# Copying the products of a seven-product matmul pair out with ScalarE and joining them as side work

## The chip, the core and the metric

The kernel runs on one core of one Trainium2 chip. A core has a matrix engine (PE, TensorE), two element-wise engines that matter here (DVE is VectorE, ACT is ScalarE), a third one (POOL, GpSimd) that does little here besides starting some transfers, and SP (SyncE), which only starts transfers between the chip's large memory and the on-chip memory SBUF. PE writes its results to PSUM, a small memory of eight banks; DVE and ACT read them from there. Each engine works through its own instructions strictly in order, and waits at an instruction until the semaphores that it needs have been raised.

The metric is the time of one execution in microseconds (us). Lower is better.

## The reference

Two layers of a hybrid decoder trunk on x of 512 positions by 2048 features, in fp32. Cut to what matters:

```python
for l in range(DEPTH):                                  # DEPTH = 2
    h = rms_norm(x, pre_norm_g[l])
    proj = jnp.einsum('bsd,de->bse', h, w_in[l])        # 2048 -> 6656
    (rq, rk, rv, rg, dq, dk, dv, dg, lx, lg) = jnp.split(proj, split_idx, axis=-1)
    ret_out  = rms_norm(retention(rq, rk, rv)) * silu(rg)               # 768 wide
    diff_out = rms_norm(diff_attention(dq, dk, dv), g) * c * silu(dg)   # 512 wide
    lru_out  = rg_lru(lx) * silu(lg)                                    # 768 wide
    mixed = jnp.concatenate([ret_out, diff_out, lru_out], axis=-1)
    y = jnp.einsum('bse,ed->bsd', mixed, w_out[l])      # 2048 -> 2048
    x = x + rms_norm(y, post_norm_g[l])
```

## The kernel before

**Products.** A matmul takes operands in a reduced fp32 format (fp32r), so every weight and activation is held as two parts, `hi` and `lo`, and one product is three matmuls: hi by hi, hi by lo, lo by hi. A weight chunk comes from memory as `raw` (128 partitions by 1024 values, 512 KB), ACT casts it to `whi` (line 190), and DVE subtracts that from `raw` to get `wlo` (line 191). `raw`, `whi` and `wlo` have three buffers each. So the buffer for the `raw` of a chunk is free only when the `wlo` of the third chunk before it has been made.

**Order of the work.** Each layer has 13 passes of the input projection, and then the output projection in four parts: pass 13 is the first 512 output columns (four PSUM banks), part 14 is the Pair (output columns 512 to 1535), and the two last passes are the last 512 columns, two banks each. `run_pass` and `run_pair` emit the matmuls (lines 296 and 370). Before each of them `ensure(i)` steps the weight chunks on: a chunk is a generator with a load, an addition (in the Pair only) and a split, and the additions run 2 chunks ahead of the splits, the loads 4. All else (norms, attention, the next layer's preparation) is side work: generators in a queue `side`, of which `pump()` runs one step between matmuls. SP's instructions run in the order in which the program wrote them; the other engines' are ordered by a scheduler by priority, and evacuations and chunk steps carry a raised priority (`HP`).

**The Pair.** The 1024 output columns are computed with seven products of half-size blocks in place of eight (the scheme of Strassen and Winograd). There are 28 units, numbered from 0: four of A11·B11, then, for four parts c, S1·T1 and S3·T3 by turns, then S2·T2 and S4·B22, then A12·B21 and A22·T4. One unit is 12 matmuls, and each product fills two PSUM banks (t = 0 and 1). The weight sides T1 to T4 are sums of weight blocks: DVE adds a `raw` to `wx` (line 230), and for S3·T3 POOL starts a transfer that adds to a `raw` in place (line 234). The activation sides S1 to S4 are made by `Sums` from `mf`, full-precision copies of the mixed activations (lines 396, 406, and 386/387 for their split). At the last part of each product `evac` takes the PSUM banks: three products are copied to SBUF by ACT (line 338), the four others are combined by DVE straight out of PSUM (lines 341, 345, 351 and 354, with 346 to 348 in SBUF). `o1`/`o2` are `out_y`: a sum of squares by ACT (line 990) and a product with the norm's weight by DVE (line 997).

**The end of a layer.** `finish` (line 1016, DVE) adds the residual `xr` to the scaled result. In the first layer it is followed by the preparation of the next layer's input: PE transposes (line 1024), ACT `hhi` (1031), DVE `hlo` (1032). The residual comes by 16 loads of 256 KB each, `load_x` (line 977), which are side work that is put in the queue at the unit (A12·B21, 0). Their tiles come from the pool `U` (77 tiles of 128 by 512).

**Turned tiles.** `diff_final` (from line 755) turns the attention's output by PE transposes into PSUM, ACT makes `mhi` from it (768), DVE `mlo` (769), and ACT makes `mf`, the same values again in plain fp32 (771).

Of the kernel before, what the change touches and what calls it, by code (L numbers as in the profile page):

```python
# [17 lines left out]
AF = mybir.ActivationFunctionType  # L18
ALU = mybir.AluOpType
# [19 lines left out]
ADD, LOAD = 2, 4  # L39
# [10 lines left out]
K_LRU, K_RET, K_DIFF = 0, 6, 12  # L50
# [63 lines left out]
A11_B11, A12_B21, S1_T1, S2_T2, S4_B22, S3_T3, A22_T4 = range(7)  # L114
# [6 lines left out]
def tile_hybrid_trunk(ctx, tc, x, xt, pos, ppar, lamqk, w_in, gw, w_out, postg, cp, cm, out):  # L121
    nc = tc.nc
# [18 lines left out]
    def U(s, dt=F32):  # L141
        return up.tile([P, S], dt, tag="u", name=nm(s))
# [70 lines left out]
    def load_unit(i):  # L213
        p, (s, c) = chunk_list[i]
        w1, w2 = p.w
        if s == A11_B11:
            src = p.x[c] = [U("wx"), U("wx")]
            for kk in range(2):
                nc.sync.dma_start(src[kk], w1[c][:, kk * S:(kk + 1) * S])
        elif s == S1_T1:  # L220
            p.kept[c] = load_raw(w2[c])
        elif s == S2_T2:
            p.kept[c] = load_raw(w2[c + 4])
        elif s == A12_B21:
            p.kept[c] = load_raw(w1[c + 4])
        yield
        if s in (S1_T1, S2_T2, A22_T4):
            src = p.x[c]
            for kk in range(2):
                V.tensor_tensor(src[kk], src[kk], p.kept[c][:, kk, :], op=ALU.add)  # L230
        elif s != A11_B11:
            src = p.kept[c]
        if s == S3_T3:
            nc.gpsimd.dma_start(src, w2[c + 4].rearrange("p (k c) -> p k c", k=2), accum_op=ALU.add)
        yield
        hi, lo = split_tiles()
        if isinstance(src, list):
            for kk in range(2):
                split(hi[:, kk, :], lo[:, kk, :], src[kk])
        else:  # L240
            split(hi, lo, src)
        chunk_tiles[i] = (hi, lo)
        yield


    def ensure(i):
        for step, more in enumerate((LOAD, ADD, 0)):
            while loaded[step] <= min(i + more, len(chunk_list) - 1):
                n = loaded[step]
                if n not in steps:  # L250
                    steps[n] = (load_unit if isinstance(chunk_list[n][0], Pair) else load_chunk)(n)
                with tc.high_priority(HP):
                    next(steps[n])
                loaded[step] += 1
# [63 lines left out]
        for c in range(nch):  # L318
            del chunk_tiles[base + c]

    def run_pair(p, begin):
        base = cbase[0]
        cbase[0] += len(UNITS)
        ps, p1, p5, p7 = {}, {}, {}, {}
        lo_, hi_ = slice(0, 256), slice(256, 512)

        def stationary(s, c, kk, part):
            if s in SUM_OF:
                return p.sums.parts[SUM_OF[s], c][part][:, kk * 256:(kk + 1) * 256]
            k = 2 * c + kk + (0 if s == A11_B11 else 8)  # L330
            return p.act[k][part][:, hi_ if s == A22_T4 else lo_]

        def evac(s, t, x):
            o1, o2 = p.out
            if s in (A11_B11, S1_T1, S3_T3):
                held = {A11_B11: p1, S1_T1: p5, S3_T3: p7}[s]
                held[t] = U("held")
                A.copy(held[t], x)
            elif s == A12_B21:
                e = U("e")  # L340
                V.tensor_tensor(e, x, p1[t], op=ALU.add)
                o1(t, e)
            elif s == S2_T2:
                w, e = U("w"), U("e")
                V.tensor_tensor(w, x, p1[t], op=ALU.subtract)
                V.tensor_tensor(p5[t], p5[t], w, op=ALU.add)
                V.tensor_tensor(e, p5[t], p7[t], op=ALU.subtract)
                V.tensor_tensor(p7[t], p7[t], w, op=ALU.subtract)
                o2(2 + t, e)
            elif s == S4_B22:  # L350
                V.tensor_tensor(p5[t], x, p5[t], op=ALU.add)
                o2(t, p5.pop(t))
            else:
                V.tensor_tensor(p7[t], x, p7[t], op=ALU.add)
                o1(2 + t, p7.pop(t))

        for n, (s, c) in enumerate(UNITS):
            if (s, c) in begin:
                side.append(begin[s, c]())
            if s in SUM_OF:  # L360
                until(lambda: (SUM_OF[s], c) in p.sums.parts)
            ensure(base + n + 2)
            hi, lo = chunk_tiles.pop(base + n)
            for t in range(2):
                if c == 0:
                    ps[s, t] = pb.tile([P, S], F32, tag="big", name=nm("big"))
                for kk in range(2):
                    ah, al = (stationary(s, c, kk, part)[:, t * P:(t + 1) * P] for part in range(2))
                    for m, (wt, at) in enumerate(((hi, ah), (hi, al), (lo, ah))):
                        T.matmul(ps[s, t], lhsT=at, rhs=wt[:, kk, :], start=(c == kk == m == 0),  # L370
                                 stop=(c == 3 and kk == 1 and m == 2))
                if c == 3:
                    with tc.high_priority(HP):
                        evac(s, t, ps.pop((s, t)))
            pump()


    class Sums:
# [10 lines left out]

        def make(self, c):  # L390
            f, plain = self.f, self.plain
            for k in (2 * c, 2 * c + 1):
                if k not in f:
                    f[k] = U("mf")
                    hi, lo = self.act[k]
                    V.tensor_tensor(f[k], hi.bitcast(F32), lo.bitcast(F32), op=ALU.add)
# [16 lines left out]
                del f[k]  # L413

        def all(self):
            for c in (0, 1, 3, 2):
                yield from self.make(c)
                yield
# [340 lines left out]
    def diff_final(l, st):  # L759
        for tb in range(NT):  # L760
            V.tensor_tensor(st["dod"][tb], st["dod"][tb], st["dg"][tb], op=ALU.mult)
        yield
        for h in range(DIFF_H):
            ps = SM("dT")
            for tb in range(NT):
                T.transpose(ps[:, tb * P:(tb + 1) * P], st["dod"][tb][:, h * P:(h + 1) * P], ident)
            hi, lo = U("mhi", F32R), U("mlo", F32R)
            A.activation(hi, ps, AF.Identity, scale=subg[:, l:l + 1])
            V.scalar_tensor_tensor(lo, ps, subg[:, l:l + 1], hi, op0=ALU.mult, op1=ALU.subtract)
            m = st["mf"][K_DIFF + h] = U("mf")  # L770
            A.activation(m, ps, AF.Identity, scale=subg[:, l:l + 1])
            st["mix"][K_DIFF + h] = (hi, lo)
            yield

# [381 lines left out]
    for l in range(DEPTH):  # L1156
# [5 lines left out]
        for i, (p, tasks) in enumerate(layer_passes[l]):  # L1162
# [4 lines left out]
                st["pg"][n] = U("pg")  # L1167
                nc.sync.dma_start(st["pg"][n], postg[l, n * S:(n + 1) * S].partition_broadcast(P))
            if isinstance(p, Pair):
                run_pair(p, {(S1_T1, 1): st["sums"].rest, (A12_B21, 0): lambda l=l, st=st: load_x(l, st)})  # L1170
            else:
                run_pass(p)
            for t in tasks:
# [98 lines left out]
```

## Time and profile before

| | us |
|---|---|
| Median of three runs (1648.52 to 1648.67) | 1648.53 |
| The profiled execution's own time | 1647.76 |
| Its span, first to last instruction | 1646.0 |
| PE busy | 1613.4 |
| DVE busy | 1048.5 |
| ACT busy | 710.4 |
| POOL busy | 66.2 |
| Mean granted clock of PE | 0.993 of full speed |
| Data moved | 181.70 MB, 110 GB/s on average |

The profile shows one execution. PE is busy in all but 32.6 us of the span, so what can be had at its present work is in these 32.6 us and in the stretches where its clock was granted at less than full speed. A row of the timeline gives the start, the duration, the engine, the line and the operation (out <- in), and in brackets how long the engine had been idle and what released it. A row of the windows gives a stretch, its length, and for each engine the busy time and the number of instructions, then the granted clock, the share of the transfer engines, and GB/s. "SPq" is SP's instruction queue.

### The profile page before, as it was taken

Reading aid. Unit: us, or ns where it says so; the run is one execution under the profiler, and the core shown is the slowest. Engines: PE = TensorE matmul, PEld = TensorE weight load, DVE = VectorE, ACT = ScalarE, POOL = GpSimd, SP = SyncE. Lnnn points to the kernel's source line nnn. Section 1 sums busy time; section 2 is a strip of 40 time slices with the busy share of each in tenths; the row PEclk is TensorE's granted clock in tenths of the full one; section 3 lists DMA queues with packets and bytes.
Section 4 is the critical chain, followed back from the end, with each engine's and each line's share of the span. In section 5 each row is a group of like instructions: output and inputs, shape, how many; then the busy total and the mean of one; then the engine's idle time right before and its main releaser. Section 6 shows DMA issues by size and latency. Waiting matters only on the chain.

```text
span 1646.0 us, 19583 instructions
## 1 busy us (share of the span) xinstructions
PE 1613.4 (98%) x7445; PEld 1326.6 (81%) x7445; DVE 1048.5 (64%) x1798; ACT 710.4 (43%) x1134; POOL 66.2 (4%) x92
## 2 busy tenths in 40 slices
PE   9999999999999999999799999999999999999997
PEld 7888888878888887877588888887888888878776
DVE  7747746557586456868662774655757744458686
ACT  7233333456732235444552343434673222435442
POOL 1010000000000000000120000000000000000001
PEclk9999999999999999999899999999999999999998
DMA  6333332223233222446543232222323322234466
GB/s 229 122 99 100 93 100 65 84 89 98 77 101 94 75 78 97 116 113 227 189 158 98 90 103 90 77 72 89 97 79 100 103 65 77 90 102 123 115 221 220
DMA packets 57053, 181.70 MB, mean 110 GB/s; under 512 B 6912, under 2 KB 7936, under 8 KB 56960
## 3 DMA queue, kind: packets, MB, share of 16 engines
q1 hardware_dynamic: 53744, 169.94, 32.3%
q0 software_dynamic: 3072, 10.49, 2.5%
q8 instruction: 58, 0.95, 0.2%
q14 instruction: 35, 0.29, 0.1%
q10 hardware_dynamic: 144, 0.04, 0.0%
HBM read 172.05 MB, written 8.39 MB: 110 GB/s over the span
## 4 chain that ended last, share of the span: by engine, by line
PE 87%; DVE 6%; issue 3%; DMA 2%; ACT 2%; POOL 0%; DVEq 0%; POOLq 0%; ACTq 0%
PE big L296 75%; PE big L370 4%; DMA raw<-in_w_out 2%; DVE wlo L191 2%; PE gate L815 1%; PE acc L706 1%; ACT whi L190 1%; PE ro L909 1%; PE rs L884 1%; PE sc L673 1%; PE sc L674 1%; PE wT L696 1%; PE ro L912 0%; PE kv L898 0%; DVE wx L230 0%
## 5 line engine op out<-in xcount | busy, mean ns | idle before, releaser
L191 DVE TENSOR_TENSOR wlo<-raw,whi 128x1024 fp32r<-128x1024 f32 (+1 forms) x281 | 340.6, 1218 | 320.1 <-ACT whi L190 315.5
L190 ACT CAST whi<-raw 128x1024 fp32r<-128x1024 f32 (+1 forms) x281 | 293.2, 1047 | 485.3 <-PE big L296 319.1
L296 PE MATMUL big<-hhi,whi 128*128 128x512 f32 x1024 | 401.8, 393 | 0.0
L296 PE MATMUL big<-hhi,wlo 128*128 128x512 f32 x1024 | 399.1, 390 | 0.0
L296 PE MATMUL big<-hlo,whi 128*128 128x512 f32 x1024 | 398.9, 390 | 0.0
L296 PE MATMUL big<-whi,hhi 128*128 128x512 f32 x640 | 253.3, 398 | 0.0
L296 PE MATMUL big<-whi,hlo 128*128 128x512 f32 x640 | 249.9, 390 | 0.0
L296 PE MATMUL big<-wlo,hhi 128*128 128x512 f32 x640 | 249.8, 391 | 0.0
L296 PEld LDWEIGHTS big<-hhi,wlo 128*128 128x128 f32 x1024 | 192.2, 188 | 40.5
L296 PEld LDWEIGHTS big<-hhi,whi 128*128 128x128 f32 x1024 | 192.5, 188 | 39.4
L296 PEld LDWEIGHTS big<-hlo,whi 128*128 128x128 f32 x1024 | 192.4, 188 | 38.8
L296 PEld LDWEIGHTS big<-wlo,hhi 128*128 128x128 f32 x640 | 120.2, 188 | 26.2 <-DVE wlo L191 0.5
L296 PEld LDWEIGHTS big<-whi,hhi 128*128 128x128 f32 x640 | 120.5, 188 | 24.1 <-ACT whi L190 1.0
L296 PEld LDWEIGHTS big<-whi,hlo 128*128 128x128 f32 x640 | 120.5, 188 | 23.8
L296 PE MATMUL big<-whi,mhi 128*128 128x512 f32 x256 | 102.4, 401 | 6.7 <-ACT whi L190 6.7
L296 PE MATMUL big<-wlo,mhi 128*128 128x512 f32 x256 | 100.6, 400 | 3.4 <-DVE wlo L191 3.2
L296 PE MATMUL big<-whi,mlo 128*128 128x512 f32 x256 | 101.2, 396 | 0.0
L682 ACT ACTIVATE pr<-sc,mx 128x128 f32<-128x128 f32 (+3 forms) x64 | 33.2, 523 | 86.6 <-DVE mx L679 86.6
L296 PEld LDWEIGHTS big<-whi,mhi 128*128 128x128 f32 x256 | 49.1, 192 | 18.1 <-ACT whi L190 8.5
L296 PEld LDWEIGHTS big<-wlo,mhi 128*128 128x128 f32 x256 | 49.3, 192 | 16.6 <-DVE wlo L191 6.3
L296 PEld LDWEIGHTS big<-whi,mlo 128*128 128x128 f32 x256 | 49.1, 192 | 9.9
L370 PE MATMUL big<-wlo,sh 128*128 128x512 f32 x128 | 50.5, 395 | 3.3 <-DVE wlo L191 3.3
(264 smaller groups left out, 1945.0 us busy)
## 6 DMA issues: line engine op xcount, KB each, us to landing
raw<-in_w_in SPq DMA_DIRECT2D x207, 512.0 KB, 3.6
raw<-in_w_out SPq DMA_DIRECT2D x72, 512.0 KB, 3.8
xT<-in_xt SPq DMA_DIRECT2D x16, 256.0 KB, 6.6
wx<-in_w_out SPq DMA_DIRECT2D x16, 256.0 KB, 4.3
raw<-in_w_out POOLq DMA_DIRECT2D x8, 512.0 KB, 6.1
xr<-in_x SPq DMA_DIRECT2D x16, 256.0 KB, 6.1
xr<-xs SPq DMA_DIRECT2D x16, 256.0 KB, 6.6
pg<-in_postg SPq DMA_DIRECT2D x8, 256.0 KB, 3.9
```

Source lines behind the costliest of these rows:

```text
L190: last_copy[0] = A.copy(hi, raw)
L191: V.tensor_tensor(lo, raw, hi, op=ALU.subtract)
L296: T.matmul(ps[b], lhsT=lhsT, rhs=rhs, start=(cnt[b] == 0), stop=(cnt[b] == total - 1))
L370: T.matmul(ps[s, t], lhsT=at, rhs=wt[:, kk, :], start=(c == kk == m == 0), stop=(c == 3 and kk == 1 and m == 2))
L673: T.matmul(ps[:, :n], lhsT=qs[:, blk], rhs=ks[:, :n], start=True, stop=False)
L674: T.matmul(ps[:, :n], lhsT=qs[:, blk], rhs=kl[:, :n], start=False, stop=True)
L682: A.activation(p[:, :n], sc[c][:, :n], AF.Exp, bias=mx[:, c:c + 1], scale=0.125, accum_out=sums[:, h:h + 1])
L696: T.transpose(ps[:, kb * P:(kb + 1) * P], w[:, kb * P:(kb + 1) * P], ident)
L706: T.matmul(accs[i][:, h * P:(h + 1) * P], lhsT=wt[:, kb * P:(kb + 1) * P], rhs=dv[kb][:, h * P:(h + 1) * P], start=(kb == 0), stop=(kb == i))
L815: T.matmul(ps[:BW, :], lhsT=wt[:BW, cols], rhs=at[:BW, :], start=(n == 0), stop=(n == 2))
L884: T.matmul(ps[:, n * P:(n + 1) * P], lhsT=k[:, n * P:(n + 1) * P], rhs=q[:, n * P:(n + 1) * P], start=True, stop=True)
L909: T.matmul(po[:, n * P:(n + 1) * P], lhsT=sT[:, n * P:(n + 1) * P], rhs=v[:, n * P:(n + 1) * P], start=True, stop=(n == 0))
```

## The change

Five things are changed, in both layers.

1. All seven products of the Pair are copied out of PSUM by ACT (`held`). They are joined by DVE from SBUF, in three generators that go to the side queue after the units number 11, 19 and 27.
2. The 16 residual loads are emitted one by one, one after each unit from number 12 on, and are no longer side work.
3. `ensure` emits the split of the chunk that is needed first, then the additions of later chunks, then the loads.
4. The transfer that adds in place is emitted at the addition step of S1·T1, not of S3·T3, on the same tile.
5. `diff_final` no longer makes `mf`; `Sums.make` makes it by a DVE addition of hi and lo. `Sums.all` begins with an empty step.

```diff
-        if s == S3_T3:
-            nc.gpsimd.dma_start(src, w2[c + 4].rearrange("p (k c) -> p k c", k=2), accum_op=ALU.add)
+        if s == S1_T1:
+            nc.gpsimd.dma_start(p.kept[c], w2[c + 4].rearrange("p (k c) -> p k c", k=2), accum_op=ALU.add)
...
-        for step, more in enumerate((LOAD, ADD, 0)):
+        for step, more in ((0, 0), (1, 0), (2, 0), (0, ADD), (1, ADD), (0, LOAD)):
...
-    def run_pair(p, begin):
+    def run_pair(p, begin, loads):
...
-        def evac(s, t, x):
-            o1, o2 = p.out
-            if s in (A11_B11, S1_T1, S3_T3):
-                held = {A11_B11: p1, S1_T1: p5, S3_T3: p7}[s]
-                held[t] = U("held")
-                A.copy(held[t], x)
-            elif s == A12_B21:
-                e = U("e")
-                V.tensor_tensor(e, x, p1[t], op=ALU.add)
-                o1(t, e)
-            elif s == S2_T2:
-                w, e = U("w"), U("e")
-                V.tensor_tensor(w, x, p1[t], op=ALU.subtract)
-                V.tensor_tensor(p5[t], p5[t], w, op=ALU.add)
-                V.tensor_tensor(e, p5[t], p7[t], op=ALU.subtract)
-                V.tensor_tensor(p7[t], p7[t], w, op=ALU.subtract)
-                o2(2 + t, e)
-            elif s == S4_B22:
-                V.tensor_tensor(p5[t], x, p5[t], op=ALU.add)
-                o2(t, p5.pop(t))
-            else:
-                V.tensor_tensor(p7[t], x, p7[t], op=ALU.add)
-                o1(2 + t, p7.pop(t))
+        held, left = {s: {} for s in range(7)}, {}
+        o1, o2 = p.out
+        def join_first():
+            p1, p5, p7 = held[A11_B11], held[S1_T1], held[S3_T3]
+            for t in range(2):
+                V.tensor_tensor(p5[t], p5[t], p1[t], op=ALU.subtract)
+                yield
+                left[t] = U("held")
+                V.tensor_tensor(left[t], p7[t], p1[t], op=ALU.add)
+                yield
+        def join_right():
+            p2, p3, p5, p7 = held[S2_T2], held[S4_B22], held[S1_T1], held[S3_T3]
+            for t in range(2):
+                V.tensor_tensor(p5[t], p5[t], p2[t], op=ALU.add)
+                V.tensor_tensor(p3[t], p3[t], p5[t], op=ALU.add)
+                yield
+                V.tensor_tensor(p5[t], p5[t], p7.pop(t), op=ALU.subtract)
+                V.tensor_tensor(left[t], left[t], p2.pop(t), op=ALU.subtract)
+                yield
+            for t in range(2):
+                o2(t, p3.pop(t))
+                yield
+                o2(2 + t, p5.pop(t))
+                yield
+        def join_left():
...
                 if c == 3:
+                    held[s][t] = U("held")
                     with tc.high_priority(HP):
-                        evac(s, t, ps.pop((s, t)))
+                        A.copy(held[s][t], ps.pop((s, t)))
+            if n in (11, 19, 27):
+                side.append({11: join_first, 19: join_right, 27: join_left}[n]())
+            if n > 11:
+                next(loads)
             pump()
...
-            for k in (2 * c, 2 * c + 1):
+            for k in (2 * c, 2 * c + 1, 2 * c + 8, 2 * c + 9):
...
         def all(self):
+            yield
...
-            m = st["mf"][K_DIFF + h] = U("mf")
-            A.activation(m, ps, AF.Identity, scale=subg[:, l:l + 1])
...
-                run_pair(p, {(S1_T1, 1): st["sums"].rest, (A12_B21, 0): lambda l=l, st=st: load_x(l, st)})
+                run_pair(p, {(S1_T1, 1): st["sums"].rest}, load_x(l, st))
```

How the instructions move, at three places. All names are the kernel's; the number behind a name counts tiles. After the change the lines have other numbers: 386 and 387 are 405 and 406, 396 is 415, 768 and 769 are 788 and 789, 977 is 995, 997 is 1015, 1016 is 1034.

**ACT, from the attention's last head to the first weight casts of pass 13** (first layer). `mhi` and `mf` are made from the turned tiles, `sh` is the cast of a sum of activations, `whi` the cast of a weight chunk. Before:

```order
L768 ACTIVATE mhi_5099<-dT_5094,subg 128x512
L771 ACTIVATE mf_5103<-dT_5094,subg 128x512
L768 ACTIVATE mhi_5110<-dT_5105,subg 128x512
L771 ACTIVATE mf_5114<-dT_5105,subg 128x512
L768 ACTIVATE mhi_5121<-dT_5116,subg 128x512
L771 ACTIVATE mf_5125<-dT_5116,subg 128x512
L768 ACTIVATE mhi_5132<-dT_5127,subg 128x512
L771 ACTIVATE mf_5136<-dT_5127,subg 128x512
L386 CAST sh_5184<-sf_5178 128x512
L386 CAST sh_5209<-sf_5181 128x512
L190 CAST whi_5146<-raw_5144 128x1024
L386 CAST sh_5228<-sf_5206 128x512
```

With the change:

```order
L788 ACTIVATE mhi_5099<-dT_5094,subg 128x512
L788 ACTIVATE mhi_5108<-dT_5103,subg 128x512
L788 ACTIVATE mhi_5117<-dT_5112,subg 128x512
L788 ACTIVATE mhi_5126<-dT_5121,subg 128x512
L405 CAST sh_5194<-sf_5188 128x512
L405 CAST sh_5213<-sf_5191 128x512
L190 CAST whi_5138<-raw_5136 128x1024
L190 CAST whi_5172<-raw_5170 128x1024
L405 CAST sh_5242<-sf_5210 128x512
```

The four `mf` are gone between the `mhi`, and the second weight cast stands ahead of the third `sh`.

**SP, at the end of the first layer.** `xr` is a residual load, `raw` a weight load. Before:

```order
L977 DMA xr_6290<-in_x 128x512
L182 DMA raw_6292<-in_w_out 128x1024
L977 DMA xr_6317<-in_x 128x512
L977 DMA xr_6490<-in_x 128x512
L182 DMA raw_6494<-in_w_out 128x1024
L182 DMA raw_6512<-in_w_out 128x1024
L182 DMA raw_6532<-in_w_out 128x1024
```

With the change, the end of the residual loads and the weight loads behind them:

```order
L182 DMA raw_6144<-in_w_out 128x1024
L995 DMA xr_6166<-in_x 128x512
L1186 DMA pg_6168<-in_postg 128x512
L182 DMA raw_6172<-in_w_out 128x1024
L182 DMA raw_6196<-in_w_out 128x1024
L182 DMA raw_6220<-in_w_out 128x1024
```

The last residual load stood 8 weight loads further on; now it stands ahead of the layer's last `pg` load, and from there on only weight loads follow.

**DVE, in the second layer's last two passes.** `wlo` is the second part of a weight chunk, L1016 (after: L1034) is `finish`. Before:

```order
L994 SCALAR_TENSOR_TENSOR sy_12694<-ssy,msy 128x1
L997 TENSOR_TENSOR y_12693<-big_12518,pg_12515 128x512
L1016 SCALAR_TENSOR_TENSOR y_11819<-y_11819,ry_12696,xr_12427 128x512
L1016 SCALAR_TENSOR_TENSOR e_12474<-e_12474,ry_12696,xr_12447 128x512
L1016 SCALAR_TENSOR_TENSOR held_12125<-held_12125,ry_12696,xr_12481 128x512
L1016 SCALAR_TENSOR_TENSOR y_12693<-y_12693,ry_12696,xr_12513 128x512
L191 TENSOR_TENSOR wlo_12714<-raw_12711,whi_12713 128x1024
```

With the change:

```order
L1012 SCALAR_TENSOR_TENSOR sy_12724<-ssy,msy 128x1
L191 TENSOR_TENSOR wlo_12742<-raw_12739,whi_12741 128x1024
L1015 TENSOR_TENSOR y_12723<-big_12538,pg_12535 128x512
L1034 SCALAR_TENSOR_TENSOR y_11825<-y_11825,ry_12726,xr_12275 128x512
L1034 SCALAR_TENSOR_TENSOR held_11977<-held_11977,ry_12726,xr_12295 128x512
L1034 SCALAR_TENSOR_TENSOR held_12343<-held_12343,ry_12726,xr_12319 128x512
L1034 SCALAR_TENSOR_TENSOR y_12723<-y_12723,ry_12726,xr_12345 128x512
L191 TENSOR_TENSOR wlo_12760<-raw_12757,whi_12759 128x1024
```

A `wlo` has moved ahead of the four `finish` additions.

More of the change, by code (lines that the diff above doesn't have):

```diff
@@ L319, in run_pass @@
             del chunk_tiles[base + c]
-    def run_pair(p, begin):
+    def run_pair(p, begin, loads):
         base = cbase[0]
         cbase[0] += len(UNITS)
-        ps, p1, p5, p7 = {}, {}, {}, {}
+        ps = {}
         lo_, hi_ = slice(0, 256), slice(256, 512)
@@ L357, in run_pair @@
+        def join_left():
+            p1, p2, p4 = held[A11_B11], held[A12_B21], held[A22_T4]
+            for t in range(2):
+                V.tensor_tensor(p1[t], p1[t], p2.pop(t), op=ALU.add)
+                o1(t, p1.pop(t))
+                yield
+                V.tensor_tensor(left[t], left[t], p4.pop(t), op=ALU.add)
+                o1(2 + t, left.pop(t))
+                yield
         for n, (s, c) in enumerate(UNITS):
@@ L415, in all @@
         def all(self):
+            yield
             for c in (0, 1, 3, 2):
```

## The prediction

> **What bounds the kernel now.** I read the busy times first, then PE's idle time by stretches, then what released PE after each gap.
>
> ```profile
> PE 1613.4 (98%) x7445; PEld 1326.6 (81%) x7445; DVE 1048.5 (64%) x1798; ACT 710.4 (43%) x1134; POOL 66.2 (4%) x92
> PE big L296 <- ACT whi L190: 6.7, 3, 3.7
> PE hT L1024 <- DVE hlo L1032: 5.4, 3, 2.7
> PE big L370 <- DVE wlo L191: 3.3, 6, 1.1
> PE big L370 <- DVE held L351: 2.1, 2, 1.0
> PE big L370 <- DVE w L345: 0.6, 2, 0.3
> ```
>
> PE is the bound: 1646.0 − 1613.4 = 32.6 us idle. The change takes no matmul away, so its gain can only come out of these waits (total, count, longest) and of slowly clocked matmuls behind them. Five places hold nearly all that the change can reach: the start of pass 13, the Pair's evacuations, its weight chunks, the end of layer 0, and the last passes of layer 1. Some 8 us at the very end, behind the last matmul, stay.
>
> **Start of pass 13: the removed `mf`.**
>
> ```profile
> 639.63 0.69 ACT L768 ACTIVATE mhi<-dT,subg 128x512 fp32r<-128x512 f32 x1 [1.94 <-PE dT L766]
> 641.14 0.69 ACT L771 ACTIVATE mf<-dT,subg 128x512 f32<-128x512 f32 x1 [0.82 <-DVE mlo L769]
> 641.72 0.68 ACT L768 ACTIVATE mhi<-dT,subg 128x512 fp32r<-128x512 f32 x1
> 651.55 0.50 PE L296 MATMUL big<-whi,mhi 128*128 128x512 f32 x1 [1.49 <-ACT whi L190]
> 653.74 0.50 PE L296 MATMUL big<-wlo,mhi 128*128 128x512 f32 x1 [0.53 <-DVE wlo L191]
> 1470.00:1475.00 5.00, 4.03 (x18) 3.00 (x16) 4.41 (x10) 2.95 (x5) 0.00 (x0) 1.00 0.01 2
> 1475.00:1480.00 5.00, 3.95 (x16) 2.97 (x17) 5.00 (x9) 1.93 (x3) 0.00 (x0) 1.00 0.25 73
> ```
>
> ACT and DVE hand each head to and fro: `mhi`, `mlo`, then `mf` on ACT, which waits 0.82 us for `mlo`, and only then the next `mhi`: 641.72 − 639.63 = 2.09 us a head. The rest (two `mf` additions, the `sf`, `sh`, the first `whi`) queues behind it, and PE stalls 1.49 + 0.53 = 2.02 us here, and (5 − 4.03) + (5 − 3.95) = 2.02 us in layer 1. Without `mf` on ACT a head needs no more than the longest of the three, about 0.7 us in place of 2.09, since the next head lies in another PSUM bank; the last one, three heads on, comes up to 3 × 1.4 = 4.2 us earlier and the `whi` with it. Late by 1.49, it would be early by some 2.7. The four `mf` become DVE additions of 0.68 us (a pair takes 1.29 in a row below) further on in the pass, behind splits that PE needs first; if they stood ahead of the first `wlo` they would give back up to 2.7. Gain 2.02 × 2 = **4.0 us**.
>
> **The Pair's evacuations.**
>
> ```profile
> 744.25 0.50 PE L370 MATMUL big<-whi,mhi 128*128 128x512 f32 x1 [0.34 <-DVE w L345]
> 747.86 0.50 PE L370 MATMUL big<-whi,mhi 128*128 128x512 f32 x1 [1.05 <-DVE held L351]
> 740.00:750.00 10.00, 8.61 (x35) 6.47 (x36) 9.96 (x16) 4.45 (x10) 0.00 (x0) 1.00 0.73 255
> 1565.00:1575.00 10.00, 8.67 (x38) 6.44 (x37) 9.96 (x17) 5.14 (x12) 0.00 (x0) 1.00 0.76 247
> 680.00:770.00 90.00, 86.78 (x376) 69.56 (x374) 71.07 (x115) 47.11 (x81) 2.63 (x3) 1.00 0.50 149
> L338 ACT COPY held<-big 128x512 f32<-128x512 f32 x6 | 3.5, 584 | 1.5 <-PE big L370 1.5
> ```
>
> Where S2·T2 and S4·B22 end, DVE works 9.96 of 10 us, the two bank reads (L345, L351) stand in its queue between joins and `wlo`, and PE waits for the bank: 0.34 + 1.05 = 1.39 us, and 10 − 8.67 = 1.33 us in layer 1. ACT is idle more than half of that stretch (4.45 of 10); a copy frees a bank in 0.584 us, and PE needs 12 × 0.227 = 2.7 us for a unit (0.227 is 20.00 us by 88 matmuls in the stretch 750 to 770, below). Gain **2.7 us**. A copy waits for its product's last matmul, and behind it on ACT stand the next casts; they are for units two further on, 5.4 us away, against 0.6 for the copy. The price: ACT makes 8 copies more and 4 `mf` fewer a layer (8 × 0.58 − 4 × 0.69 = 1.9 us), DVE 16 joins for 14 and 4 `mf` additions more (6 × 0.68 = 4.1 us). In the 90 us around the Pair DVE has 90 − 71 = 19 us free and the joins are no longer urgent: nothing on the path. Uncovered, it would be 2 × 4.1 = 8.2 us.
>
> **The Pair's weight chunks (splits first, the earlier in-place addition).**
>
> ```profile
> 737.50 1.29 DVE L230 TENSOR_TENSOR wx<-wx,raw 128x512 f32<-128x512 f32 x2 [3.21 <-DMA raw<-in_w_out]
> 700.00:740.00 40.00, 38.17 (x167) 30.46 (x165) 25.82 (x37) 19.92 (x29) 0.86 (x1) 1.00 0.41 115
> 750.00:770.00 20.00, 20.00 (x88) 16.06 (x86) 18.21 (x34) 10.90 (x20) 0.00 (x0) 1.00 0.52 175
> raw<-in_w_out SPq DMA_DIRECT2D x72, 512.0 KB, 3.8
> raw<-in_w_out POOLq DMA_DIRECT2D x8, 512.0 KB, 6.1
> ```
>
> The six waits of PE on a `wlo` come to 3.3 us in both layers. A `wlo` that PE needs stands on DVE behind an addition that waits for its `raw`; that `raw` could be asked for only when an earlier `wlo` had freed a buffer: a ring of three. In the changed order the waiting addition still precedes the `wlo` at most of these places, because DVE is ordered by priority and both have the same one. The ring stays, and the in-place transfer (6.1 us) still waits for the addition that reads the same tile. Bounds: all 3.3 us gone, or as much again. I take **0**.
>
> **The end of layer 0: the residual loads.**
>
> ```profile
> SPq L977 <- DVE hlo L1032: 15.4, 1, 15.4
> 781.90 15.97 SPq L977 DMA_DIRECT2D xr<-in_x  x2
> 797.99 1.69 SPq L182 DMA_DIRECT2D raw<-in_w_out  x3
> 803.78 1.12 PE L1024 MATMUL hT<-cmt,y 128*128 128x128 f32 x4 [2.71 <-DVE hlo L1032]
> 808.64 0.79 PE L296 MATMUL big<-whi,mhi 128*128 128x512 f32 x1 [3.75 <-ACT whi L190]
> 815.12 0.39 PE L296 MATMUL big<-wlo,mhi 128*128 128x512 f32 x1
> 795.00:815.00 20.00, 10.77 (x39) 7.32 (x38) 12.86 (x32) 14.10 (x40) 2.09 (x4) 0.66 0.66 216
> 785.00:850.00 65.00, 55.48 (x253) 43.35 (x252) 47.03 (x104) 44.41 (x118) 14.48 (x26) 0.89 0.49 168
> 826.00:850.00 24.00, 23.86 (x120) 19.27 (x119) 20.77 (x50) 19.63 (x56) 8.32 (x15) 1.00 0.44 154
> ```
>
> This is the largest hole. The last residual load waited 15.4 us in SP's queue for a tile that only the tail of the layer frees, and every weight load behind it waited too, until 797.99. PE has 20 − 10.77 = 9.23 us idle, and then 15 matmuls from 808.64 to 815.12, 6.48 us where 15 × 0.227 = 3.41 would do: 3.07 more at a granted clock of 0.5. Together 12.3 us. In the changed queue the residual loads lie within the Pair and none of them waits there for DVE. The weight loads come when the ring allows, PE has matmuls to do while `finish`, `hhi` and `hlo` run, and the hole closes, but not for nothing: 47.0 us of DVE and 44.4 of ACT must now fit in 65 − 12.3 = 52.7 us, 89% and 84% busy. The stretch 826 to 850 has such loads (20.77 and 19.63 of 24) and PE full. I count **12.3 us**, and 2 us back for new short waits.
>
> **The last passes of layer 1.**
>
> ```profile
> 1616.73 0.75 DVE L1016 SCALAR_TENSOR_TENSOR y<-y,ry,xr 128x512 f32<-128x512 f32 x1 [0.79 <-POOL ry L996]
> 1619.39 3.48 DVE L191 TENSOR_TENSOR wlo<-raw,whi 128x1024 fp32r<-128x1024 f32 x3
> 1620.66 0.80 PE L296 MATMUL big<-wlo,mhi 128*128 128x512 f32 x1 [2.17 <-DVE wlo L191]
> 1624.13 0.40 PE L296 MATMUL big<-whi,mhi 128*128 128x512 f32 x1
> 1615.00:1625.00 10.00, 7.83 (x28) 6.05 (x27) 7.08 (x10) 2.10 (x2) 3.77 (x7) 0.83 0.91 300
> ```
>
> A `wlo` stood behind four `finish` additions (1616.73 to 1619.39); PE lost 2.17 us, and 8 matmuls took 1624.13 − 1620.66 = 3.47 us for 1.82: 3.8 us. In the changed queue one `wlo` stands ahead of the four, and the residual loads no longer share the transfer engines here (0.91 busy). Gain **3.8 us**. Page and row differ on the second part: the Trainium skill ("TensorE: Matmul & The Clock Gate", "HAM oscillation — how this bites in real kernels") says the clock falls after idle gaps above about 3.4 us. By it this gap of 2.17 us would cost no slow matmuls, and the sum would be 1.65 us smaller; the row shows 0.43 us a matmul behind it, and the row goes.
>
> **Sum.** 4.0 + 2.7 + 0 + 12.3 + 3.8 = 22.8 us, less 2 us at the layer's end and 1 us in the Pair for residual loads between weight loads: 20 us. The profiled execution took 1647.76, which gives 1628 of its kind; the runs' median is 0.8 above it, so **1628.5**.
>
> **Rivals.**
>
> *The residual loads starve the Pair (slower).*
>
> ```profile
> xr<-in_x SPq DMA_DIRECT2D x16, 256.0 KB, 6.1
> 741.47 3.76 SPq L977 DMA_DIRECT2D xr<-in_x  x6
> ```
>
> Ten of the sixteen now lie ahead of or between six weight loads in SP's order, in a Pair that already lives from load to load. Each weight load could land as late as a residual load does, or behind it: from 3.8 to 6.1, and with the ring in the path each delay reaches PE, and the following one (two loads between two weights) doubles it. At 2 × 2.3 = 4.6 us on 6 loads in two layers: +55, less 22.8: 1681. It decides from 22.8 / 12 = 1.9 us per load on. A page speaks for it: the Trainium skill ("DMA: Bandwidth & Descriptors", "Issuing engines are not separate DMA queues") says that transfers of all engines run on the same 16 DMA engines and interleave. Against it: from 750 to 770 residual and weight loads alternate already, and PE is busy 20.00 of 20 us.
>
> *The layer's end only moves.* DVE and ACT at 84 to 89% hand `hhi` and `hlo` to and fro; PE's transposes wait for `hlo` as now (5.4 us in three waits) while only the wait for the late cast goes (3.75). That keeps the 5.4 us and the 3.1 us of slow matmuls behind them: gain 22.8 − 5.4 − 3.1 − 1 = 13.3, **1635**. For it: the three hT waits in the profile. Against: at present they come as a burst, with no matmuls ready in between.
>
> *The chunk edits do more than I give them.* If the Pair's 3.3 us go and nothing comes back: 22.8 + 3.3 = 26.1 us, **1622.5**.
>
> *The change does not do what it says:* the `whi` of pass 13 and the joins stay as late as they are (−4.0 − 2.7 and 3 us of new waits): 1648.5 − 22.8 + 9.7 = **1635.5**, by another road.
>
> **Chances.** My forecast (gain 17 to 24) 0.57; the layer's end only moves 0.18; chunk edits gain 0.10; evacuation and `mf` bring nothing 0.06; starving 0.06, most of it slower; no change, from mixtures of these, 0.03. Range **1621.5 to 1640**: below, all five terms with the chunk waits; above, the moved hole with up to 5 us lost in the Pair. One measurement tells 0.2% (3.3 us) from no change: faster 0.92, within 0.03, slower 0.05.
>
> **What would show it.** Right: no gap at the first `whi` of pass 13; no wait of PE on L345 or L351's successors, and the ACT copies at 0.58 us; the weight loads at the end of layer 0 issued steadily from 770 to 800, with no SP wait on `hlo`; granted clock 1.00 in the stretch 795 to 815 and in the last passes. Wrong: waits of `big` on `wlo` inside the Pair above 3.3 us, weight loads landing later than 4 us there; or an hT wait on `hlo` with the same 5 us.

## The result, and the profile after

| | before | after |
|---|---|---|
| Median, us | 1648.53 (1646.02 to 1648.67) | 1627.4 (1627.17 to 1628.52) |
| Profiled execution: span, us | 1646.0 | 1625.3 |
| PE busy, us | 1613.4 | 1607.0 |
| PE idle in the span, us | 32.6 | 18.3 |
| Mean granted clock | 0.993 | 0.997 |

The ratio is 0.9877, with a 95% interval of 0.986 to 0.9894: 1.2% faster. Of the 20.7 us of span, 14.3 are idle time of PE and 6.4 are busy time, which the profile models longer behind a gap and at a slow clock.

A stall therefore costs more than the idle time that the profile shows for it. Where PE waited 1.49 us at 651.55 in the kernel before, the matmul ahead had begun at 649.67 and the next one began 0.34 us later: 1.88 and 0.34 us where 0.227 each would do, so 1.76 us were lost. These extra 0.27 us come with every wait between two matmuls of 128x512 in both profiles; where slow matmuls follow it is more.

First the busy row and the waits of PE in the profile after (total, count, longest). Lines have the new numbers: 384 is the Pair's matmul, 296 that of the other passes.

```profile
PE 1607.0 (99%) x7445; PEld 1324.6 (81%) x7445; DVE 1055.3 (65%) x1810; ACT 713.1 (44%) x1142; POOL 67.5 (4%) x92
PE big L384 <- ACT whi L190: 3.0, 2, 2.1
PE big L384 <- DVE wlo L191: 2.5, 4, 1.2
PE big L296 <- DVE wlo L191: 1.0, 3, 0.5
PE big L296 <- ACT whi L190: 0.7, 3, 0.3
PE hT L1042 <- DVE y L1034: 0.2, 1, 0.2
```

The wait of the transposes for `hlo` (5.4 us) and both bank waits (2.1 and 0.6) are gone, and the wait of the ordinary passes for `whi` has gone from 6.7 to 0.7. In the Pair, though, PE now waits 5.5 us for weight parts where it waited 3.3.

The windows of the profile after (stretch, length, then busy time and count of PE, PEld, DVE, ACT, POOL, then granted clock, share of the transfer engines, GB/s):

```profile
700.00:740.00 40.00, 37.17 (x159) 29.17 (x158) 28.44 (x40) 21.05 (x32) 0.57 (x1) 1.00 0.53 150
740.00:750.00 10.00, 10.00 (x45) 8.26 (x44) 9.47 (x16) 6.73 (x13) 0.00 (x0) 1.00 0.93 308
795.00:815.00 20.00, 20.00 (x100) 16.05 (x99) 17.83 (x39) 18.36 (x49) 2.23 (x5) 1.00 0.64 200
1505.00:1515.00 10.00, 7.84 (x27) 5.61 (x27) 6.98 (x10) 4.59 (x7) 1.79 (x3) 0.83 0.96 181
```

The stretch 795 to 815, which lost 9.23 us and ran at a clock of 0.66, is full at 1.00, and with DVE and ACT at 89 and 92%. The stretch 740 to 750 is full too. Within the first Pair the stretch 700 to 740 is worse than it was (37.17 of 40 against 38.17), and a new slow place has come up at 1505 in the second layer.

The stages in both profiles, bounded by the starts of the first and the last matmul of each Pair and of the program's last matmul:

| stage | before, us | after, us | difference | the prediction's terms there |
|---|---|---|---|---|
| start to the Pair of layer 0 | 685.15 | 682.44 | −2.7 | −2.0 |
| Pair of layer 0 | 80.76 | 80.26 | −0.5 | −1.4 + 0.5 |
| to the Pair of layer 1 | 743.21 | 726.92 | −16.3 | −12.3 + 2 − 2.0 |
| Pair of layer 1 | 80.37 | 81.26 | +0.9 | −1.3 + 0.5 |
| to the last matmul | 48.06 | 46.00 | −2.1 | −3.8 |
| sum | | | −20.7 | −19.8 |

The first row is uncertain by about a us: p_pg and p_pg_b below are the same program and reach the first Pair at 683.60 and 682.48.

### The profile page after: what moved, and what is told of

It is laid out like the page before. It is cut to its first block, busy times and chain, and to the rows that moved or that the text cites. A ratio compares the mean times of both kernels' runs of the same rounds, so it can differ in the third digit from the quotient of the medians.

```text
span 1625.3 us, 19623 instructions
## 1 busy us (share of the span) xinstructions
PE 1607.0 (99%) x7445; PEld 1324.6 (81%) x7445; DVE 1055.3 (65%) x1810; ACT 713.1 (44%) x1142; POOL 67.5 (4%) x92
## 4 chain that ended last, share of the span: by engine, by line
PE 91%; DVE 3%; DMA 2%; issue 1%; ACT 1%; POOL 0%; DVEq 0%; POOLq 0%; ACTq 0%
PE big L296 78%; PE big L384 6%; DMA raw<-in_w_out 2%; DVE wlo L191 2%; PE gate L833 1%; PE acc L726 1%; PE ro L927 1%; PE rs L902 1%; PE sc L693 1%; PE sc L694 1%; ACT whi L190 1%; PE wT L716 1%; PE ro L930 0%; PE kv L916 0%; PE hT L1042 0%
## 5 line engine op out<-in xcount | busy, mean ns | idle before, releaser
L384 PE MATMUL big<-whi,sh 128*128 128x512 f32 x128 | 50.7, 396 | 3.0 <-ACT whi L190 3.0
```

## The experiments

The kernel before took a median of 1645.3 to 1648.5 us on the different chips, so kernels of different sets are compared by their ratio to the kernel before beside them, and in detail by their traces. Set 1 is u_evac, u_mf, u_order and d_xr; set 2 a_same, p_pg, p_pg_o and d_mf; set 3 p_pg_b, p_evac, q_w2 and x_late. In the names u is the change with a part undone, d the kernel before with one part alone, p and q the change with something added; a_same is the change again, and x_late the change with one load moved.

| kernel | median, us | kernel before beside it | ratio (95%) |
|---|---|---|---|
| u_evac | 1626.89 | 1646.07 | 0.9885 (0.9865 to 0.9904) |
| u_mf | 1628.85 | 1646.07 | 0.9890 (0.9874 to 0.9906) |
| u_order | 1625.79 | 1646.07 | 0.9873 (0.9858 to 0.9887) |
| d_xr | 1630.97 | 1646.07 | 0.9905 (0.9891 to 0.9920) |
| a_same | 1625.64 | 1645.32 | 0.9878 (0.9859 to 0.9898) |
| p_pg | 1621.47 | 1645.32 | 0.9854 (0.9836 to 0.9871) |
| p_pg_o | 1621.94 | 1645.32 | 0.9856 (0.9838 to 0.9874) |
| d_mf | 1638.80 | 1645.32 | 0.9953 (0.9937 to 0.9969) |
| p_pg_b | 1621.01 | 1647.56 | 0.9851 (0.9834 to 0.9868) |
| p_evac | 1625.57 | 1647.56 | 0.9872 (0.9857 to 0.9886) |
| q_w2 | 1641.51 | 1647.56 | 0.9968 (0.9956 to 0.9980) |
| x_late | 1623.36 | 1647.56 | 0.9867 (0.9847 to 0.9887) |

### d_xr: the residual loads alone

```diff
-                run_pair(p, {(S1_T1, 1): st["sums"].rest, (A12_B21, 0): lambda l=l, st=st: load_x(l, st)})
+                run_pair(p, {(S1_T1, 1): st["sums"].rest}, load_x(l, st))
...
+            if n > 11:
+                next(loads)
```

> The kernel before with the second part alone: one residual load after each unit from number 12 on. Theory (the hole at the end of layer 0 comes from the last residual load in SP's queue and the weight loads behind it): PE full from 795 to 815 at granted clock 1.00, 1648.5 - 12.3 = 1636.2; if the second layer's late wlo also comes from the residual loads (by the transfers that they share), 3.8 less, 1632.4. Rival (the layer's end only moves, PE waits for hlo as before): 1641 to 1645. Rival (the loads starve the Pair): above 1640, with raw loads landing later than 6 us in it.

It took 15.1 us less than the kernel before (1646.07 − 1630.97; 13.2 to 17.9 by the interval), three quarters of the whole gain. Its windows and waits (here the transpose is line 1026):

```profile
795.00:815.00 20.00, 19.04 (x94) 15.14 (x93) 16.70 (x38) 18.40 (x49) 2.72 (x5) 1.00 0.64 220
1600.00:1615.00 15.00, 14.47 (x64) 11.53 (x63) 10.69 (x14) 5.26 (x5) 4.07 (x7) 1.00 0.76 277
PE hT L1026 <- DVE hlo L1034: 1.0, 1, 1.0
PE big L370 <- DVE wlo L191: 1.3, 1, 1.3
```

The hole at the end of layer 0 is down to 0.96 us and the clock stays at 1.00. The rival in which the transposes keep waiting for `hlo` falls: 1.0 us is left of 5.4. The rival that the loads starve the Pair falls as well: the waits on `wlo` in it are 1.3 us, less than before (3.3), both Pairs are shorter (80.1 and 78.8 us for 80.8 and 80.4), and weight loads land in 3.4 and 3.6 us at the median there, where the kernel before has 3.6 and 4.2.

The second layer's late `wlo` goes with it, from 2.17 to 0.53 us. The expectation put that down to the transfers which the residual loads share. A row of the kernel before speaks for another cause, the order on DVE:

```profile
1613.92 1.06 ACT L190 CAST whi<-raw 128x1024 fp32r<-128x1024 f32 x1 [0.99 <-DMA raw<-in_w_out]
```

The `raw` of that chunk had landed by 1613.92 and its `whi` was made by 1614.98. DVE then stood idle for 0.79 us, made the four `finish` additions, and took up the `wlo` only at 1619.39. In d_xr a `wlo` at 1600.88 stands ahead of the four (1602.62 to 1605.35).

### x_late: one residual load late

```diff
-            if n > 11:
+            if 11 < n < 27:
                 next(loads)
...
             ensure(base + max(c, n // nb) + 2)
+            if late is not None and n == 8:
+                next(late)
             mm(c, b)
```

> The changed kernel with one load moved: the last residual load of each layer is emitted in the pass behind the Pair, five weight loads further on. Theory (a residual load that waits in SP's queue for a tile of U holds up the weight loads behind it): SP waits there, the weight loads behind it are issued some us later, and PE stalls at the end of the first layer by 2 us or more, 1629 to 1636 where the changed kernel has 1626 to 1627. Rival (a tile is free at that place, and only the moving of all sixteen loads mattered): SP does not wait there, and the time stays within 1 us.

Here the rival was right. The load goes out at once, between the weight loads of SP's queue:

```profile
765.92 3.50 SPq L182 DMA_DIRECT2D raw<-in_w_out  x3
769.54 0.36 SPq L997 DMA_DIRECT2D xr<-in_x  x1
771.48 23.82 SPq L182 DMA_DIRECT2D raw<-in_w_out  x9
```

No wait, and PE is full from 790 to 830. So a late place in the queue does no harm by itself; the harm in the kernel before came from a load that reached the head of the queue while no tile of `U` was free for it (15.4 us). Whoever moves such loads moves them to where a tile is free. The ratio, 0.9867, can't be told from the change's. No run puts the load where the kernel before had it, eight weight loads further on.

### d_mf and u_mf: `mf` of the turned tiles

d_mf is the kernel before with this, u_mf the change with the reverse; the empty first step of `Sums.all` is not in d_mf, and stays in u_mf:

```diff
-            m = st["mf"][K_DIFF + h] = U("mf")
-            A.activation(m, ps, AF.Identity, scale=subg[:, l:l + 1])
...
-            for k in (2 * c, 2 * c + 1):
+            for k in (2 * c, 2 * c + 1, 2 * c + 8, 2 * c + 9):
```

> The kernel before with the fifth part alone, less the empty step: mf of the turned tiles by DVE. Theory of the prediction: PE's wait at the start of pass 13 gone in both layers, 4.0 us less than the kernel before. Rival (formed after the first four runs: PE then reaches the Pair 2 us earlier, but the in-place transfers do not come earlier, so that most of it is waited out there): 1 to 2 us less, with the waits at the first S3T3 unit above 1.5 us.

> The changed kernel with the fifth part undone: ACT makes mf of the turned tiles again, DVE no longer adds them. Theory (the to and fro of mhi, mlo and mf set the first weight cast of pass 13): PE's wait of about 2.0 us at the start of pass 13 is back in both layers, 1627.4 + 4.0 = 1631.4 (1630.5 to 1632.5). Rival (the empty first step of Sums and the new order of splits had already brought the cast ahead): no wait there, 1627.4 within 0.8.

The first row is u_mf's at the first `whi` of pass 13, the other two are d_mf's for the same place and for its waits in the Pair:

```profile
651.52 0.50 PE L296 MATMUL big<-whi,mhi 128*128 128x512 f32 x1 [1.49 <-ACT whi L190]
```

```profile
650.00:655.00 5.00, 5.00 (x24) 4.14 (x23) 4.98 (x10) 1.39 (x2) 0.00 (x0) 1.00 0.86 303
PE big L370 <- DVE wlo L191: 1.1, 3, 0.7
```

The mechanism stands: with `mf` on ACT the stall is there (1.49 us in each layer; the second one of 0.53 does not come back), without it PE is full. In d_mf the first `whi` of the pass begins at 646.73 in place of 650.46, 3.7 us earlier, where the prediction had 4.2 at most.

The size depends on the surroundings. Alone, the part brings 6.5 us (1645.32 − 1638.80; 5.1 to 10.4 by the interval): the two stalls in each layer, 4.0 us of idle time and 5.1 with what comes with each stall, and 2.2 less waiting for `wlo` in the Pair (3.3 before, 1.1 here). Undone in the change it costs about 2 (0.9890 against 0.9878, within the intervals) and not the 4.0 expected. In its trace PE waits less in the Pair, 3.5 us for `whi` and `wlo` against 6.0 in a_same; that execution was the fastest of its four (1626.55, the others 1628.17 to 1629.58).

The unit that the expectations call the first S3·T3 unit is by the traces number 7, the second of the four. The rival for d_mf, that PE would wait out the gain there, is wrong: PE reaches the Pair 2.6 us earlier (682.57 against 685.15), and its waits at unit 7 go down, to 0.21 and 0.25 us from 0.53 and 0.30.

### u_evac and p_evac: the copies by ACT

Both undo the first part, u_evac in the change, p_evac in p_pg (below). Shown is the place of the copies alone; `evac` is that of the kernel before, and the joins go:

```diff
-                    held[s][t] = U("held")
                     with tc.high_priority(HP):
-                        A.copy(held[s][t], ps.pop((s, t)))
-            if n in (11, 19, 27):
-                side.append({11: join_first, 19: join_right, 27: join_left}[n]())
+                        evac(s, t, ps.pop((s, t)))
```

> The changed kernel with its first part undone: S2T2, S4B22, A12B21 and A22T4 are again combined by DVE out of PSUM, all else as changed. Theory (the bank waits for DVE were worth 2.7 us, and a copy by ACT takes them off the path): PE waits again some 0.3 + 1.0 us for the bank reads by DVE where S2T2 and S4B22 end, in each layer, and the time is 1627.4 + 2.7 = 1630.1 (1629 to 1631.5). Rival (the other parts already unload DVE there, so that the copies bring nothing): no such wait, 1627.4 within 0.8.

> The kernel with the two pg loads moved into the Pair, with the first part of the change undone: S2T2, S4B22, A12B21 and A22T4 combined by DVE out of PSUM. When that part was undone with the pg loads ahead of the Pair, PE's waits for the bank reads came back (2.7 us), and other waits in the Pair went down by about as much. Theory (late weights of the first S3T3 unit took the slack there; with SP free the banks count in full): 2 to 3 us more than the reference beside it. Rival (the ring of three raw buffers bounds the Pair as a whole, so that a wait for a bank is only taken out of a later wait for wlo): within 1 us, with bank waits of 2.7 us and 2 us less in waits for wlo.

Waits of PE in u_evac, and then in p_evac:

```profile
PE big L370 <- DVE wlo L191: 2.2, 5, 0.6
PE big L370 <- ACT whi L190: 2.2, 2, 1.1
PE big L370 <- DVE held L351: 2.1, 2, 1.0
PE big L370 <- DVE w L345: 0.7, 2, 0.3
```

```profile
PE big L370 <- DVE wlo L191: 2.4, 4, 0.9
PE big L370 <- DVE held L351: 2.0, 2, 1.0
PE big L370 <- DVE w L345: 1.5, 2, 0.8
```

In u_evac the bank waits are back as expected, 2.8 us, but the waits for weight parts are 4.4 in place of a_same's 6.0, and the 1.0 of the first chunks behind the Pair is gone. The net cost is at most some 1 us (0.9885 against 0.9878, inside the intervals). So in the change as it stands the copies pay next to nothing: what PE does not wait for a bank it waits for a weight. In p_evac, where the weights are no longer late at the start of the Pair, the bank waits are 3.5 us and the kernel takes 4.6 us more than its reference (1625.57 − 1621.01). Not all of it is the copies': of the 4.4 us between the two profiled executions 1.0 lies ahead of the Pair (683.46 against 682.48), where the first 50 us ran at a granted clock of 0.97 against 1.00. That leaves about 3.5, somewhat more than the 2 to 3 expected. So the theory was right there, and the rival, that the ring of buffers swallows the gain in any case, was not.

### u_order: the old order of `ensure`, and the old place of the in-place transfer

```diff
-        if s == S1_T1:
-            nc.gpsimd.dma_start(p.kept[c], ...
+        if s == S3_T3:
+            nc.gpsimd.dma_start(src, ...
...
-        for step, more in ((0, 0), (1, 0), (2, 0), (0, ADD), (1, ADD), (0, LOAD)):
+        for step, more in enumerate((LOAD, ADD, 0)):
```

> The changed kernel with parts three and four undone: loads first, then additions, then splits, and the in-place transfer at S3T3. Theory of the prediction (these two change nothing, the ring of three raw buffers sets the waits in the Pair): 1627.4 within 1.0, the same waits of PE on whi and wlo in the Pair (5.5 us). Rival A (they gained as meant): the Pair's waits grow, 1629 to 1631. Rival B (the in-place transfers, three within 4 us, now slow each other and are what PE waits for at the first S3T3 unit, 1.4 us in the first layer and 2.1 with slow matmuls in the second): 1624 to 1626.

0.9873 against 0.9878 for the change: no difference that can be told. Waits in the Pair are 4.6 us, and those at unit 7 are no shorter than with the change (1.42 + 0.53 us in the first layer, 1.41 + 0.53 in the second). So the early emission of the transfer is not what makes it late there, and rival B falls; nor did the two parts gain anything that can be told, so rival A falls too.

### a_same, p_pg, p_pg_b and p_pg_o: what makes the in-place transfers late

In the profile after, SP, POOL, ACT and PE show this around the Pair's start in the first layer, and, in the last rows, PE in the second:

```profile
SPq L1186 <- DVE y L1015: 28.4, 1, 28.4
657.82 0.33 SPq L182 DMA_DIRECT2D raw<-in_w_out  x1
686.65 1.87 SPq L1186 DMA_DIRECT2D pg<-in_postg  x2
688.61 18.43 SPq L182 DMA_DIRECT2D raw<-in_w_out  x5
696.07 0.89 POOL L234 DMA_DIRECT2D raw<-in_w_out  x1 [19.60 <-ACT whi L190]
702.55 0.50 PE L384 MATMUL big<-whi,sh 128*128 128x512 f32 x1 [0.91 <-ACT whi L190]
1510.94 0.80 PE L384 MATMUL big<-whi,sh 128*128 128x512 f32 x1 [2.12 <-ACT whi L190]
1514.42 0.39 PE L384 MATMUL big<-whi,sl 128*128 128x512 f32 x1
```

From 658 to 686 SP stands still: the loads of two norm weights (`pg`) wait 28.4 us for a tile of `U`, and all the Pair's loads of `raw` but the first stand behind them. The weights land, DVE adds, and only then can POOL start the in-place transfers of the second to the fourth S3·T3 unit. The one started at 696.07 is cast when PE already waits at unit 7. It is the trap of the residual loads again, 110 us earlier.

The kernel before has this wait too:

```profile
SPq L1168 <- DVE sl L387: 21.4, 1, 21.4
686.61 1.53 SPq L1168 DMA_DIRECT2D pg<-in_postg  x2
```

There PE lost only 0.53 us at unit 7. That PE now comes earlier is not the reason: in d_mf it does too, and it loses less. What has changed is when the tile comes free. The first `pg` load goes out 1.45 us behind the Pair's first matmul in the kernel before and in d_xr, 2.27 in d_mf, 3.93 in u_mf, and 4.2 in the change, in u_evac and in u_order. So the first, third and fourth parts do not make it late, nor does the second by itself. The fifth is left, and of it mainly the empty first step of `Sums.all`, which u_mf has and d_mf lacks. No run takes out that step by itself, so this is inferred and not shown.

The `pg` are not needed before the joins, so p_pg emits them in the Pair:

```diff
-            for n in {13: (0,), 14: (1, 2), 15: (3,)}.get(i, ()):
+            for n in {13: (0,), 15: (3,)}.get(i, ()):
...
+            if n in (12, 13):
+                pg = st["pg"][n - 11] = U("pg")
+                nc.sync.dma_start(pg, postg[l, (n - 11) * S:(n - 10) * S].partition_broadcast(P))
             if n > 11:
                 next(loads)
```

> The changed kernel itself, unaltered, beside the next three on one chip, since the kernel before took 2.5 us less on the chip of the last four runs than on the first: 0.9877 of the kernel before, within the interval already seen (0.986 to 0.9894).

> The changed kernel with the loads of the Pair's two norm weights (pg 1 and 2) emitted in the Pair, after the units 12 and 13, in place of ahead of it. In the changed kernel these two loads wait in SP's queue 28.4 us for a tile of the pool U, with the Pair's first weight loads behind them. Theory (this wait is what makes the first in-place transfers late): weight loads are issued by 675 in place of 688.6, PE's waits at the first S3T3 unit (0.91 + 0.53 us, and 2.12 us with slow matmuls behind it in the second layer) are gone: 4 to 5 us less than the unaltered kernel beside it. Rival (the ring of three raw buffers or the in-place transfer itself sets them): the waits stay above 1 us, the same time within 0.8.

> The changed kernel with the two pg loads moved into the Pair, again, as the reference on this chip for the next two: 0.9854 of the kernel before within the interval seen (0.9836 to 0.9871).

> The same move of the two pg loads, with parts three and four undone (loads first, splits last, the in-place transfer at S3T3). Theory (parts three and four matter by a us at most, and the other waits on wlo in the Pair, 1.15 and 0.56 us, come from additions that stand ahead of the split on DVE, which the old order of emission does not make worse): within 1 us of the kernel with pg moved alone. Rival (the early in-place transfer pays once SP is free): 2 us or more slower than it.

SP and POOL in p_pg, and PE's waits there:

```profile
658.99 50.49 SPq L182 DMA_DIRECT2D raw<-in_w_out  x6
687.36 0.90 POOL L234 DMA_DIRECT2D raw<-in_w_out  x1 [9.73 <-ACT whi L190]
PE big L384 <- DVE wlo L191: 2.9, 5, 1.2
```

Two of the weight loads that stood behind `pg` go out at 664.20 and 669.64, where the change has 688.61 and 689.10. The in-place transfer for unit 7 starts at 687.36 in place of 696 to 697, PE waits for no `whi` in the Pair (2.4 us in a_same), and the second layer's Pair takes 77.0 us in place of 80.1. The time is 4.2 us below the change beside it (1625.64 − 1621.47), as expected, and its four runs (1620.84 to 1622.58) all lie below the lowest of a_same (1623.45); the second set of runs gives 0.9851. This version is faster than both kernels of the case, at 0.985 of the kernel before. The old order of `ensure` and of the transfer (p_pg_o) makes no difference here either (0.9856).

### q_w2: a fourth buffer for `raw`

```diff
-        raw = wp.tile([P, 2, S], F32, tag="raw", name=nm("raw"))
+        raw = wp.tile([P, 2, S], F32, tag="raw", name=nm("raw"), bufs=4)
...
-                wp.tile([P, 2, S], F32R, tag="wlo", name=nm("wlo")))
+                wp.tile([P, 2, S], F32R, tag="wlo", name=nm("wlo"), bufs=2))
```

> The kernel with the two pg loads moved into the Pair, and four buffers of raw in place of three; the space comes from wlo, which has two in place of three. Theory (the waits on wlo in the Pair, 2.9 us in all, come from weight loads that can be asked for only when an earlier wlo has freed a buffer): those waits go down below 1 us, DVE's additions no longer wait for raw, 1.5 to 3 us less than the reference. Rival (the splits themselves come too late, now with two buffers of wlo later still): as many waits on wlo or more, in the Pair and in other passes, 0 to 10 us more.

As a version it loses 20 us, so as a test it is only half of one. What DVE's additions (line 230) waited for their `raw`, in us and times, first in p_pg_b, then in q_w2:

```profile
  DMA raw<-in_w_out: 23.6, 12
```

```profile
  DMA raw<-in_w_out: 7.9, 8
```

The additions wait for their `raw` a third as long, and from 722 to the end of the first layer's Pair PE waits for nothing, where p_pg_b has waits of 0.82 and 0.89 us on `wlo`. That speaks for the ring of three as the cause of those two. It does not show it: other waits have come up in the Pair (1.9 us for a `y` of DVE, 1.0 for `whi`), and the two Pairs take 79.9 and 79.4 us, against 79.5 and 76.8 in p_pg_b. And the missing third `wlo` costs more, at the program's start (7.4 of the first 50 us idle, against 2.1) and elsewhere, and the Pair's total of waits for `wlo` is still 1.8 us. A fourth `raw` without taking a `wlo` away, for lack of space, wasn't tried.

## Why the prediction was right

It forecast 1628.5 and 1627.4 came out. By its own steps:

- **Start of pass 13, 4.0 us.** Right in its mechanism: PE has no gap there. What it had not seen is that each stall costs 0.27 us beside its idle time (5.1 us in all), that this part also relieves the Pair when it stands alone (6.5 us), and that with its empty step the tile for `pg` comes free later.
- **The Pair's evacuations, 2.7 us.** The bank waits went as said, and came back as said in u_evac. The step that failed is "nothing on the path" behind it: the Pair had a second limit close by. Net, the copies are worth about 1 us or less in the change and about 3.5 us once that limit is moved.
- **The chunk edits, 0.** Right: u_order and p_pg_o can't be told from their references. But "1 us in the Pair" was too little for what the Pair gave back: waits on `whi` and `wlo` 5.5 us for 3.3, 7 slow matmuls (1510.94 to 1514.42, 3.48 us for 1.59), and 0.95 us at the first chunk behind it. The named cause, residual loads between weight loads, was wrong too: d_xr has them, and its Pairs are shorter than before. p_pg shows that what PE waits for at unit 7 is the wait of `pg` in SP's queue. The row was in the profile before (21.4 us). I had asked what the residual loads would be queued ahead of, and not what already stood ahead of the Pair's loads, nor when its tile would come free.
- **The end of layer 0, 12.3 us less 2.** The largest term, and right; d_xr shows that it comes from the residual loads alone. The 2 us for new short waits were not needed: 20.00 of 20 busy, and in a_same one wait of 0.64. The mechanism was told too coarsely: by the 15.4 us of the kernel before and x_late, which has none, the tile decides and not the place in the queue.
- **The last passes of layer 1, 3.8 us.** Gaps of 0.30 and 0.53 are left there, and 0.5 at the start of these passes: 2.1 us came out in the profile after, 2.3 in a_same. Of the two causes named, the order on DVE is the one that the traces bear out.

So the total is right in part by luck: two errors of size cancel. The layer's end gave some 4 us more than counted, the Pair and the last passes gave back about as much. The mechanism of the largest term was no luck.

Two of the signs that were named misled. The sign "no SP wait on `hlo`" did not come: between 765 and 815 SP's weight loads still waited four times on it, 14.2 us in all, and PE was full even so. And the waits of `big` on `wlo` in the Pair stayed below 3.3 us (2.5), while those on `whi`, which the sign left out, came up with 3.0.

Of the rivals, starving is refuted by d_xr: with all residual loads in the Pair the weight loads there land no later than before. The page of the Trainium skill that spoke for it ("DMA: Bandwidth & Descriptors", "Issuing engines are not separate DMA queues") is not contradicted, since transfers do share, but the share was affordable. That the layer's end only moves is refuted too.

## What to carry to other kernels

An in-order queue that issues loads is stopped by the first load whose destination is not free. Look down that queue for loads of things needed late, and ask of each when its tile comes free and what stands behind it; here two such places cost 12 and 4 us, and neither showed as a busy resource. A change that moves side work also moves the times at which tiles come free, and with them the loads that wait for a tile: look for the chain that was only just in time, since it can become the next stall. An edit that pays next to nothing today (the copies by ACT) may pay in full once that chain is moved. And when stalls are added up, each costs somewhat more than the idle time that is shown for it (0.27 us here).

## What was not expected of the hardware

Slow matmuls came behind gaps shorter than I would have thought. Behind 2.12 us in the profile after, 2.17 in the one before and 2.18 in d_mf, matmuls took 0.43 us each for a while in place of 0.227. The length of the gap alone does not decide it. In the first layer of u_order waits of 1.42 and 0.53 us, with two matmuls between them, were followed by eight such matmuls, while 1.41 and 0.53 in its second layer, and 1.49 and 0.53 in the kernel before, were followed by none. In d_mf and u_order the slow ones do not begin at once. d_mf, and then u_order with the window in which its granted clock was 0.50:

```profile
1611.75 0.50 PE L296 MATMUL big<-wlo,mhi 128*128 128x512 f32 x1 [2.18 <-DVE wlo L191]
1612.32 0.46 PE L296 MATMUL big<-whi,mlo 128*128 128x512 f32 x1
1613.43 0.63 PE L296 MATMUL big<-whi,mhi 128*128 128x512 f32 x1
1615.96 0.40 PE L296 MATMUL big<-whi,mhi 128*128 128x512 f32 x1
```

```profile
703.89 0.50 PE L384 MATMUL big<-whi,sh 128*128 128x512 f32 x1 [1.42 <-ACT whi L190]
705.15 0.50 PE L384 MATMUL big<-wlo,sh 128*128 128x512 f32 x1 [0.53 <-DVE wlo L191]
705.72 0.63 PE L384 MATMUL big<-whi,sl 128*128 128x512 f32 x1
709.12 0.40 PE L384 MATMUL big<-whi,sh 128*128 128x512 f32 x1
706.00:708.00 2.00, 2.00 (x6) 1.52 (x6) 2.00 (x4) 1.38 (x3) 0.00 (x0) 0.50 1.00 272
```

The Trainium skill ("TensorE: Matmul & The Clock Gate", "The HAM clock gate (the "warmup" mystery)") says that the window over which activity is judged runs freely, and has 3.4 us as its length. The varying point at which the slow matmuls begin agrees with the first, and so does it that equal gaps are followed by slow matmuls once and not again; gaps of 2.1 to 2.2 us that bring them, and less in u_order, do not agree with a whole window of idleness.
